# A planner's waiting times for non-urgent transfers, and new ordering weights for attention, in a hybrid DeltaNet and attention layer

## The chip, the cores and the metric

The kernel runs on one core of one Trainium2 chip, in one launch. The metric is the device time of one execution in microseconds. A core has five engines that matter here: PE (TensorE, matrix products and transposes), DVE (VectorE), ACT (ScalarE), POOL (GpSimd) and SP (SyncE, which here only issues the transfers). Each takes its instructions strictly in the order of its own program; an instruction that waits for something holds up all that stand behind it on that engine.

## The reference

One layer over 1024 latent tokens and 256 context tokens with 1024 channels, all in fp32:

```
h  = rms_norm(x) * (1 + scale) + shift            # scale, shift, gate from c
cols = h @ w_in                                   # q,k,v,z of branch A; q,k,v,z of branch B; gates
A: q,k,v = silu(centred_conv(.)); l2 norm of q, k; chunked gated delta rule, both directions, 8 heads
B: q,k = axial_rope(rms_norm(.)); attn = softmax(q0 k0) - lam * softmax(q1 k1); o = attn @ v, 8 heads
y  = rms_norm(o) * gain * silu(z)                 # for each branch
out = x + gate * ((g_a * (y_a @ w_oa) + g_b * (y_b @ w_ob)) @ w_out)
```

## The kernel before

**The planner.** The program is written by a planner in Python. Each piece of work is a generator (a "stream") that yields one operation at a time: the engine, an assumed duration, the tokens it depends on, and a function that emits the instruction. A token is a pair of engine and assumed end. `step` (line 127) keeps an assumed clock for each engine, for DMA the sum of the assumed transfer times with 2.5 us for the landing on top (`LAND`), and `turn_flow` and `flow` choose which stream goes next: the one that can start first by these clocks, with a bias for each stream. The order of choice is the order of the instructions on each engine. `later(t, us)` (line 229) returns a token whose assumed end is `us` later. It changes nothing that the chip waits for: the dependency itself stays as it was, only the place that the planner gives to the instruction in its engine's program moves.

**The stages**, with their times in the trace. Modulation, norm and the first products (0 to 60 us). The projections that feed the convolution, with convolution, norms and tables on the other engines (60 to 410): `gate_row` sums a gate row out of 16 transfers `graw`. The q, k, v projections of branch B, with the preparation of the first DeltaNet heads (410 to 745): `gdn_prep` loads `X` and `kq`, forms decays on ACT and Gram products on PE, solves 32x32 triangles on DVE from `ab`, merges them from `R`. The DeltaNet scan of both directions, with 32 output-gate projections as filler for PE (745 to 1310): `loads` fetches blocks `x` and masks them on POOL, `tails` norms a head's output with the gate `sz`. Attention (1350 to 1823), with the products `ma` of branch A (`merge_`) between. Then the products `mb` of branch B and the output projection (to 1993).

**Attention** works through 64 tiles of 128 queries (8 heads of 8). A tile: 12 score products `s` on PE, six pieces taken off by DVE (`score_out`, line 1560, tile `S`), exponentials on ACT (`soft`, 1573), scaling of the second map on ACT or POOL (`scale`, 1590 and 1592), the sum of both maps on POOL (`add`, 1597), ten transposes `t` on PE (`turns`), copies of high parts on ACT (`high`, 1629) and low parts on DVE (`low`, 1634), products `v` for pairs of tiles (`att_out`). After a pair, `gate_` (1671) multiplies by the gate `sz`. After the last pair of a head, `norm_` runs a chain: POOL takes a power into `bry` (179), PE transposes it into `m`, DVE copies it to `rt`, SP writes it to memory (`rbd<-rt`, 1715), SP reads it back to all partitions (`rr<-rbd`, 1717) once that has landed, POOL multiplies the head's output by it in four pieces (`oT`, 1720), SP stores it (`yb<-oT`). `merge_` takes one of 16 groups of 24 products `ma` at a time, loads its gate `g<-gt` (1791) as the group begins, and `merge_out` multiplies by it on DVE (1806). `att_load_ops` and `att_low_ops` load a later head by six transfers (`qh`, `kk`, `qh`, `kk`, `ql`, `ql`), called the head load below.

In attention every queue above is a stream with its own weight in `ABIAS`, and a due time that grows by one for each tile; a lower weight means that the stream is taken earlier. `flow`, which plans the DeltaNet stages, adds `FB0` or `FB1` to the filler's start, `FB0` while fewer than `FT` = 38 gate projections are done; there are 32 of them.

Of the kernel before, what the change touches and what calls it, by code (L numbers as in the profile page):

```python
# [17 lines left out]
P = 128  # L18
# [25 lines left out]
class Block:  # L44
# [427 lines left out]
    def first(self, done, right, late):  # L472

        self.head = self.late = None
        yield done
        for st in right:
            st.close()
        self.late = self.tk = late()
        self.gdn_first()
        g = self.preps(0)  # L480
        x = next(g)
        while x() if callable(x) else x[0] == DMA:
            x = next(g) if callable(x) else g.send((yield x))
# [175 lines left out]
    def gate_row(self):  # L659
# [24 lines left out]

# [398 lines left out]
    def gdn_prep(self, h):  # L1083
# [18 lines left out]
        for d in range(2):  # L1102
            for c in range(NT):
                t = yield ACT, 0.293, [ld], lambda: nc.scalar.activation(
                    X[:, d, c], X[:, d, c], AF.Abs, bias=self.gcc[:, c, d * H + h:d * H + h + 1], scale=-1.0)
            te[d] = yield ACT, 1.18, [t], lambda: nc.scalar.activation(X[:, d], X[:, d], AF.Exp, scale=-1.0), AF.Exp
# [45 lines left out]
        for j in range(31):  # L1152
            n, w = 31 - j, j + 1
            tv = tmp[:, :n * w].rearrange("p (a b) -> p a b", b=w)
            t = yield DV2, n * w / 960.0 + 0.08, [t, t1], lambda: V.tensor_tensor(  # L1155
# [9 lines left out]
        tt = yield DVE, 0.735, [tR], lambda: V.transpose(Rt, R)  # L1165
# [104 lines left out]
    def loads(self, d):  # L1270
# [3 lines left out]
        for h in range(H):  # L1274
            for c in order:
# [5 lines left out]
                if c < NL:  # L1281
                    u["tqk"] = yield POOL, 0.72, [u["tx"]], lambda: nc.gpsimd.tensor_tensor(  # L1282
# [77 lines left out]
    def tails(self):  # L1360
# [3 lines left out]
        for h in range(H):  # L1364
# [23 lines left out]
            for b0 in range(0, NL, 4):  # L1388
# [10 lines left out]
                sq = yield DVE, 0.663, [t1, ts], lambda: V.scalar_tensor_tensor(  # L1399
# [82 lines left out]
    FB1 = 0.71  # L1482
# [217 lines left out]
    def norm_(self, h, w, t, to):  # L1700
# [17 lines left out]
        for k in range(4):  # L1718
            s = slice(k * W, (k + 1) * W)
            t = yield POOL, 0.69, [e, to], lambda: nc.gpsimd.tensor_tensor(w["oT"][:, s], w["oT"][:, s], rr[:, s], ALU.mult)  # L1720
# [9 lines left out]
    def side_start(self):  # L1730
# [74 lines left out]
    def merge_out(self, o, m, g, tg, pt, t):  # L1805
        t = yield DVE, 0.605, [t, tg], lambda: self.nc.vector.tensor_tensor(g, pt, g, ALU.mult)
# [396 lines left out]
```

## Time and profile before

| what | before |
|---|---|
| median of 3 runs | 1991.84 us (1985.76 to 1995.66) |
| the profiled execution, its own time | 1994.94 us |
| its span, first to last instruction | 1993.2 us |
| busy in the span: PE, DVE, ACT, POOL | 1920.1, 1462.8, 1062.0, 680.2 us |
| mean granted clock of TensorE | 0.989 |
| DMA, mean over the span | 169 GB/s |

The own time of the profiled execution is 1.74 us above its span and 3.10 us above the median. In the views below, a row of the timeline gives start, length, engine, line, operation, out<-in and, in brackets, the idle time before it with what ended that; a row of the waits gives who waited for whom, the sum, how often and the longest; a row of the windows gives the busy time of each engine in a stretch, then the granted clock (PEclk), the busy share of the DMA engines and GB/s.

### The profile page before, as it was taken

The numbers are of one execution on the slowest core, as the hardware profiler recorded it, in microseconds if no ns is written. First come the engines' busy times: TensorE is split into PE (matmuls) and PEld (weight loads), VectorE is DVE, ScalarE is ACT, GpSimd is POOL, SyncE is SP. The second block draws the span as 40 slices with busy tenths as digits, with TensorE's granted clock in tenths as the row PEclk, the third lists the DMA queues.
The fourth block names the chain that finished last, engine by engine and source line by source line (L and its number), as shares of the span: only waits on it lengthen the run. The fifth ranks groups of instructions, "written<-read, shape, count | busy, mean of one in ns | idle before, by whom it ended". The sixth has DMA issues, their size and how long they took to land.

```text
span 1993.2 us, 37530 instructions
## 1 busy us (share of the span) xinstructions
PE 1920.1 (96%) x13807; PEld 1689.6 (85%) x13807; DVE 1462.8 (73%) x3613; ACT 1062.0 (53%) x2186; POOL 680.2 (34%) x610
## 2 busy tenths in 40 slices
PE   6999999999999999999999999999899999999999
PEld 4988888899999997888888888888879879898887
DVE  4787899847976986768866873346669788895677
ACT  4443335344325443677555655456658678684222
POOL 3200000014531332343433233334657476663203
PEclk9999999999999999999999999999999999999999
DMA  9145444576455456667587576575474665426542
GB/s 325 59 131 122 133 97 121 128 220 184 125 158 186 140 195 188 222 189 245 165 281 243 157 219 194 156 203 175 128 196 113 183 181 139 142 69 209 188 159 85
DMA packets 383038, 336.39 MB, mean 169 GB/s; under 512 B 142609, under 2 KB 323443, under 8 KB 381831
## 3 DMA queue, kind: packets, MB, share of 16 engines
q1 hardware_dynamic: 382855, 333.99, 56.4%
q8 instruction: 109, 1.79, 0.4%
q14 instruction: 74, 0.61, 0.1%
HBM read 222.14 MB, written 111.79 MB: 168 GB/s over the span
## 4 chain that ended last, share of the span: by engine, by line
PE 51%; DMA 6%; DVE 2%; POOL 1%; ACT 1%; issue 1%; SPq 1%; DVEq 0%; ACTq 0%; POOLq 0%
PE mm L56 15%; PE s L56 6%; PE chain L56 5%; PE v L56 5%; PE mb L56 4%; PE ma L56 3%; PE x L56 3%; PE t L63 3%; PE out L56 3%; DMA rbd<-rt 1%; DMA x<-xq 1%; DMA g<-gt 1%; PE gram L56 1%; PE pz L56 1%; PE z L56 1%
## 5 line engine op out<-in xcount | busy, mean ns | idle before, releaser
L56 PE MATMUL mm<-hs,wh 128*128 128x512 f32 (+1 forms) x2048 | 650.3, 391 | 1.5 <-DVE hs L408 1.4
L56 PEld LDWEIGHTS mm<-hs,wh 128*128 128x128 f32 x2048 | 372.2, 190 | 59.7 <-issue 2.3
L56 PE MATMUL mm<-hs,wl 128*128 128x512 f32 (+1 forms) x1024 | 397.6, 388 | 0.0
L56 PE MATMUL mm<-wh,hs 128*128 128x256 f32 (+1 forms) x1792 | 335.9, 287 | 1.0 <-issue 0.5
L56 PEld LDWEIGHTS mm<-wh,hs 128*128 128x128 f32 x1792 | 283.2, 193 | 1.7 <-ACT sq L978 0.7
L1560 DVE TENSOR_SCALAR_CACHE_REDUCE S<-s,rsq 128x512 f32<-128x512 f32 (+1 forms) x384 | 241.5, 655 | 29.0 <-PE s L56 24.5
L56 PE MATMUL mm<-wl,hs 128*128 128x256 f32 (+1 forms) x896 | 256.7, 286 | 0.0
L56 PEld LDWEIGHTS mm<-hs,wl 128*128 128x128 f32 x1024 | 194.3, 190 | 27.9 <-DVE wl L886 0.2
L1597 POOL TENSOR_TENSOR S<-S 128x1280 f32<-128x1280 f32 x64 | 189.3, 2962 | 75.3 <-ACT S L1590 72.1
L1573 ACT ACTIVATE S<-S,mn 128x1280 f32<-128x1280 f32 x128 | 175.3, 1370 | 44.7 <-DVE mn L1572 43.7
L56 PEld LDWEIGHTS mm<-wl,hs 128*128 128x128 f32 x896 | 172.6, 193 | 0.0
L56 PE MATMUL s<-kk,qh 128*128 128x512 f32 (+1 forms) x384 | 145.5, 379 | 5.9 <-DVE S L1560 5.8
L595 DVE SCALAR_TENSOR_TENSOR ac<-xc,convT,ac 128x1284 f32<-128x1284 f32 (+1 forms) x96 | 138.4, 1446 | 12.4 <-ACT ac L593 11.9
L56 PE MATMUL s<-kk,ql 128*128 128x512 f32 (+1 forms) x384 | 135.4, 362 | 0.0
L1634 DVE TENSOR_TENSOR al<-t,ah 128x512 fp32r<-128x512 f32 (+1 forms) x192 | 108.1, 595 | 36.3 <-ACT ah L1629 36.1
L1155 DVE TENSOR_TENSOR tmp<-ab,ts 80x31 f32<-80x31 f32 (+15 forms) x248 | 98.0, 395 | 12.4 <-DMA ab<-da 6.7
L580 POOL MEMSET xc<- 128x2 f32 (+1 forms) x64 | 3.6, 101 | 299.5 <-DMA gkk<-xc 128.2
L1629 ACT CAST ah<-t 128x512 fp32r<-128x512 f32 (+1 forms) x192 | 91.7, 518 | 26.5 <-PE v L56 12.6
L63 PE MATMUL t<-ct,S 128*128 128x128 f32 x640 | 97.0, 277 | 4.4 <-POOL S L1597 2.0
L1157 DVE TENSOR_TENSOR ts<-ts,tmp 80x31 f32<-80x31 f32 (+15 forms) x248 | 93.4, 376 | 5.6
L1318 ACT ACTIVATE vd<-chain,edk 128x128 f32<-128x128 f32 x144 | 52.4, 369 | 81.6 <-PE chain L56 80.5
L1282 POOL TENSOR_TENSOR x<-x,ct 128x256 f32<-128x256 f32 x64 | 49.0, 770 | 131.1 <-DMA x<-xq 95.8
(296 smaller groups left out, 4401.4 us busy)
## 6 DMA issues: line engine op xcount, KB each, us to landing
wr<-in_w_in_dram SPq DMA_DIRECT2D x48, 512.0 KB
hx<-in_w_in_dram SPq DMA_DIRECT2D x64, 256.0 KB
x<-xq SPq DMA_DIRECT2D x64, 256.0 KB
X<-gcd SPq DMA_DIRECT2D x8, 1280.0 KB
kd<-col SPq DMA_DIRECT2D x40, 256.0 KB
xq<-X SPq DMA_DIRECT2D x16, 640.0 KB
kk<-kd SPq DMA_DIRECT2D x16, 640.0 KB
kq<-gkq SPq DMA_DIRECT2D x8, 1152.0 KB
```

Of the source, the lines that this page charges most:

```text
L56: self.nc.tensor.matmul(out, lhsT, rhs, start=start, stop=stop)
L63: self.nc.tensor.transpose(out, src, self.ident[:src.shape[0], :src.shape[0]])
L595: t = yield DV2, 1.21e-3 * wd, [t], lambda: nc.vector.scalar_tensor_tensor(ac[:, :wd], xc[:, j:j + wd], self.convw(j, x["ct"]), ac[:, :wd] ...
L1155: t = yield DV2, n * w / 960.0 + 0.08, [t, t1], lambda: V.tensor_tensor(tv, ab[:, j + 1:, j:j + 1].to_broadcast([80, n, w]), ts[:, j, :w]. ...
L1157: t = yield DV2, n * w / 960.0 + 0.08, [t, t1], lambda: V.tensor_tensor(ts[:, j + 1:, :w], ts[:, j + 1:, :w], tv, ALU.subtract)
L1282: u["tqk"] = yield POOL, 0.72, [u["tx"]], lambda: nc.gpsimd.tensor_tensor(x[:, 1], x[:, 1], (self.up, self.lo)[d].unsqueeze(1).to_broadcas ...
L1318: td = yield ACT, 0.251, [t], lambda: nc.scalar.activation(vd, pc[:, 1], AF.Copy, scale=self.edk[:, c, g:g + 1])
L1560: e = yield DVE, 0.675 if m == 512 else 0.408, [e, self.sfree[c].get(n - 4 + c)], lambda: self.nc.vector.tensor_scalar(x["S"][c][:, o:o + ...
L1573: x["x"].append((yield ACT, 1.36, [e], lambda: nc.scalar.activation(S, S, AF.Exp, bias=x["mn"][:, c:c + 1], scale=-1.0, accum_out=w["l0"][ ...
L1597: e = yield POOL, 2.9, [e], lambda: self.nc.gpsimd.tensor_tensor(S0, S0, S1, ALU.add)
L1629: e = yield ACT, 0.48 if nb == 4 else 0.27, [t, y["old", k]], lambda: self.nc.scalar.copy(y["ah", k][:, :, q], pv)
L1634: t = yield DVE, 0.603 if k < 2 else 0.322, [e, y["old", k]], lambda: self.nc.vector.tensor_tensor(y["al", k][:, :, q], pv, y["ah", k][:, ...
```

## The change

Nine kinds of operation that consume a transfer get a later place by `later`: the Gram products and their partners behind `kq` (1.5 us), the decays on ACT behind `X` (2.0), the first step of the triangles behind `ab` (2.5), the transpose behind `R` (2.5), the masks on POOL behind `x` (1.0), the gated norm of branch A behind `sz` (1.5), the gate of attention behind its `sz` (2.0), the multiplications `oT` on POOL behind `rr` (4.0), and the multiplication on DVE behind `g` (3.0). The allowance for `graw` goes from 6.0 to 4.0. The rope table `tb` is fetched before the first preparation, not after it. Five of the weights in `ABIAS` are new, and `FB1` goes from 0.71 to 0.36.

```diff
@@ first
         self.late = self.tk = late()
+        tb = self.tk.tile([P, 2, 2, NL, 32], F32, tag="tb", name="tb")
+        self.rope["k"] = tb, (yield DMA, 1.5, [], lambda: self.nc.sync.dma_start(..., self.tbd[1]))
         self.gdn_first()
...
-        tb = self.tk.tile([P, 2, 2, NL, 32], F32, tag="tb", name="tb")
-        self.rope["k"] = tb, (yield DMA, 1.5, [], lambda: self.nc.sync.dma_start(..., self.tbd[1]))
@@ gate_row
-                e = self.later(e, 6.0)
+                e = self.later(e, 4.0)
@@ gdn_prep
-            tk = tq = yield DMA, 3.3, self.kT_t, lambda: nc.sync.dma_start(kq, self.gkq[h])
+            tk = yield DMA, 3.3, self.kT_t, lambda: nc.sync.dma_start(kq, self.gkq[h])
+            tk = tq = self.later(tk, 1.5)
...
-                t = yield ACT, 0.293, [ld], lambda: nc.scalar.activation(
+                t = yield ACT, 0.293, [self.later(ld, 2.0)], lambda: nc.scalar.activation(
...
-            t = yield DV2, n * w / 960.0 + 0.08, [t, t1], lambda: V.tensor_tensor(
+            t = yield DV2, n * w / 960.0 + 0.08, [t if j else self.later(t, 2.5), t1], lambda: V.tensor_tensor(
...
-        tt = yield DVE, 0.735, [tR], lambda: V.transpose(Rt, R)
+        tt = yield DVE, 0.735, [self.later(tR, 2.5)], lambda: V.transpose(Rt, R)
@@ loads
-                    u["tqk"] = yield POOL, 0.72, [u["tx"]], ...
+                    u["tqk"] = yield POOL, 0.72, [self.later(u["tx"], 1.0)], ...
@@ tails
-                sq = yield DVE, 0.663, [t1, ts], ...
+                sq = yield DVE, 0.663, [t1, self.later(ts, 1.5)], ...
@@
-    FB1 = 0.71
+    FB1 = 0.36
@@ gate_
-        y["o"] = yield DVE, 0.345, [t, self.kept.get(h - 2), w["tsz"]], ...
+        y["o"] = yield DVE, 0.345, [t, self.kept.get(h - 2), self.later(w["tsz"], 2.0)], ...
@@ norm_
-            t = yield POOL, 0.69, [e, to], lambda: nc.gpsimd.tensor_tensor(w["oT"][:, s], w["oT"][:, s], rr[:, s], ALU.mult)
+            t = yield POOL, 0.69, [self.later(e, 4.0), to], lambda: nc.gpsimd.tensor_tensor(w["oT"][:, s], w["oT"][:, s], rr[:, s], ALU.mult)
@@
-    ABIAS = dict(rels=-0.59, softs=10.8, norms=5.82, gateq=-13.3, sums=-14.54,
+    ABIAS = dict(rels=-0.59, softs=8.84, norms=5.82, gateq=-27.29, sums=-14.54,
...
@@ merge_out
-        t = yield DVE, 0.605, [t, tg], lambda: self.nc.vector.tensor_tensor(g, pt, g, ALU.mult)
+        t = yield DVE, 0.605, [t, self.later(tg, 3.0)], lambda: self.nc.vector.tensor_tensor(g, pt, g, ALU.mult)
```

In the rest of the table `outs` goes from -50.16 to -42.85, `highs` from -18.9 to -9.33 and `att_out` from 4.51 to 8.18.

**Where instructions stand now.** The first place is SP's program around the norm chain of the first head (`rbd<-rt`, `rr<-rbd`); `qh`, `kk` and `ql` are a head load, `wq` weights, `ma` and `g` belong to the groups of `merge_`. Before:

```order
L1498 DMA kk<-kd 64x2x1280
L1506 DMA ql<-qd 64x2x1024 x2
L1808 DMA ma<-g 128x512
L1791 DMA g<-gt 128x512
L1715 DMA rbd<-rt 8x128
L1767 DMA wq<-in_w_oa_dram 128x4x128 x2
L1717 DMA rr<-rbd 128x1024
L1525 DMA vh<-vd 128x4x128
```

In the changed kernel the same place reads:

```order
L1698 DMA sz<-szb 128x1024
L1808 DMA ma<-g 128x512
L1791 DMA g<-gt 128x512
L1715 DMA rbd<-rt 8x128
L1717 DMA rr<-rbd 128x1024
L1767 DMA wq<-in_w_oa_dram 128x4x128 x2
L1726 DMA yb<-oT 128x1024
L1497 DMA qh<-qd 64x2x1024
```

The write and the read of the norm chain stood behind a head load, and stand ahead of it now. Over all eight heads, `rbd` stands right behind a head load (with only `ma` and `g` between) for heads 0 and 2 before and for none now, and a head load stands between `rbd` and `rr` for head 4 before and for head 3 now.

The second place is POOL's program from the first head's `bry` to the second head's; `S<-S` is the sum of a tile's two maps, `wl` the low part of a weight of branch A. Before:

```order
L179 TENSOR_TENSOR bry<-ms,mhalf 128x8
L1592 TENSOR_TENSOR S<-S,rl 128x1280
L1597 TENSOR_TENSOR S<-S 128x1280 x3
L1777 TENSOR_TENSOR wl<-wq,wh 128x512
L1597 TENSOR_TENSOR S<-S 128x1280
L1777 TENSOR_TENSOR wl<-wq,wh 128x512
L1720 TENSOR_TENSOR oT<-oT,rr 128x256 x4
L179 TENSOR_TENSOR bry<-ms,mhalf 128x8
```

In the changed kernel:

```order
L179 TENSOR_TENSOR bry<-ms,mhalf 128x8
L1597 TENSOR_TENSOR S<-S 128x1280
L1777 TENSOR_TENSOR wl<-wq,wh 128x512 x2
L1597 TENSOR_TENSOR S<-S 128x1280
L1720 TENSOR_TENSOR oT<-oT,rr 128x256 x4
L1597 TENSOR_TENSOR S<-S 128x1280
L1592 TENSOR_TENSOR S<-S,rl 128x1280
L1597 TENSOR_TENSOR S<-S 128x1280 x2
L1777 TENSOR_TENSOR wl<-wq,wh 128x512 x2
L1597 TENSOR_TENSOR S<-S 128x1280 x3
L179 TENSOR_TENSOR bry<-ms,mhalf 128x8
```

Before, the second head's `bry` stood right behind the first head's `oT`, and now six sums stand between. Before, `bry` of heads 1, 3 and 5 stood at most two instructions behind an `oT`; now that of head 4 does, with two `wl` between.

The third place is DVE's program around the first multiplication by `g`; the rows of line 1560 take score pieces off, 60 of them ahead of `g` before and 59 now. Before:

```order
L1560 TENSOR_SCALAR S,m_15776<-s,rsq 128x512
L1560 TENSOR_SCALAR S,m_15776<-s,rsq 128x256
L1572 TENSOR_REDUCE mn<-m_15776 128x1
L1581 RECIPROCAL rl<-l_15666 128x1
L1806 TENSOR_TENSOR g<-ma,g 128x512
L1583 TENSOR_SCALAR rl<-rl,l_15666,neglam 128x1
L1560 TENSOR_SCALAR S,m_15864<-s,rsq 128x512 x2
```

In the changed kernel:

```order
L1572 TENSOR_REDUCE mn<-m_15813 128x1
L1560 TENSOR_SCALAR S,m_15813<-s,rsq 128x512
L1806 TENSOR_TENSOR g<-ma,g 128x512
L1560 TENSOR_SCALAR S,m_15813<-s,rsq 128x256
L1560 TENSOR_SCALAR S,m_15859<-s,rsq 128x512
L1581 RECIPROCAL rl<-l_15663 128x1
```

Counted in score pieces the multiplication has hardly moved; on PE, though, a whole group of 24 products `ma` and 70 transposes now stand ahead of the 60th score piece, where 12 and 60 stood before.

More of the change, by code (lines that the diff above doesn't have):

```diff
@@ L478, in first @@
         self.late = self.tk = late()
+        tb = self.tk.tile([P, 2, 2, NL, 32], F32, tag="tb", name="tb")
+        self.rope["k"] = tb, (yield DMA, 1.5, [], lambda: self.nc.sync.dma_start(tb.rearrange("p a b t f -> p (a b t f)"), self.tbd[1]))
         self.gdn_first()
@@ L483, in first @@
             x = next(g) if callable(x) else g.send((yield x))
-        tb = self.tk.tile([P, 2, 2, NL, 32], F32, tag="tb", name="tb")
-        self.rope["k"] = tb, (yield DMA, 1.5, [], lambda: self.nc.sync.dma_start(tb.rearrange("p a b t f -> p (a b t f)"), self.tbd[1]))
         self.head = g, x
@@ L1281, in loads @@
                 if c < NL:
-                    u["tqk"] = yield POOL, 0.72, [u["tx"]], lambda: nc.gpsimd.tensor_tensor(
+                    u["tqk"] = yield POOL, 0.72, [self.later(u["tx"], 1.0)], lambda: nc.gpsimd.tensor_tensor(
                         x[:, 1], x[:, 1], (self.up, self.lo)[d].unsqueeze(1).to_broadcast([P, 2, P]), ALU.mult)
@@ L1398, in tails @@
                     t1 = yield PE, 0.109, [t, b], lambda: self.tr(pt[:, j * P:(j + 1) * P], oa[:, b0 + j])
-                sq = yield DVE, 0.663, [t1, ts], lambda: V.scalar_tensor_tensor(
+                sq = yield DVE, 0.663, [t1, self.later(ts, 1.5)], lambda: V.scalar_tensor_tensor(
                     ov, pt, self.gdn_g, sz, ALU.mult, ALU.mult)
@@ L1670, in gate_ @@
         yield lambda: "tsz" in w
-        y["o"] = yield DVE, 0.345, [t, self.kept.get(h - 2), w["tsz"]], lambda: self.nc.vector.scalar_tensor_tensor(
+        y["o"] = yield DVE, 0.345, [t, self.kept.get(h - 2), self.later(w["tsz"], 2.0)], lambda: self.nc.vector.scalar_tensor_tensor(
             w["oT"][:, s], po[:, :W], self.dg, w["sz"][:, s], ALU.mult, ALU.mult)
@@ L1743 @@
     PACE = 4.48
-    ABIAS = dict(rels=-0.59, softs=10.8, norms=5.82, gateq=-13.3, sums=-14.54,
-                 outs=-50.16, lows=-2.4, highs=-18.9, adds=26.02, scales=31.0, evs=22.29, mouts=-3.31,
-                 att_out=4.51, turns=3.19, scores=-12.11, merge=1.0)
+    ABIAS = dict(rels=-0.59, softs=8.84, norms=5.82, gateq=-27.29, sums=-14.54,
+                 outs=-42.85, lows=-2.4, highs=-9.33, adds=26.02, scales=31.0, evs=22.29, mouts=-3.31,
+                 att_out=8.18, turns=3.19, scores=-12.11, merge=1.0)
     KEEP = 3
```

## The prediction

> **What bounds the kernel now.** I read the page first, then the windows by stage, then the waits of PE, and last the timelines around the longest of them. The page and the windows say that PE sets the time almost everywhere (the columns are the stretch, then the busy time of PE, its weight loads, DVE, ACT and POOL, the clock, DMA).
>
> ```profile
> PE 1920.1 (96%) x13807; PEld 1689.6 (85%) x13807; DVE 1462.8 (73%) x3613; ACT 1062.0 (53%) x2186; POOL 680.2 (34%) x610
> ```
>
> ```profile
> 60.00:410.00 350.00, 347.85 (x1868) 299.68 (x1867) 295.80 (x444) 147.67 (x186) 7.92 (x69) 1.00 0.47 119
> ...
> 745.00:1310.00 565.00, 547.40 (x4736) 474.71 (x4735) 368.52 (x1054) 326.19 (x958) 192.45 (x248) 0.99 0.66 206
> ...
> 1350.00:1823.00 473.00, 450.91 (x2874) 398.27 (x2873) 376.11 (x1247) 347.26 (x584) 284.16 (x143) 0.97 0.55 151
> 1823.00:1993.00 170.00, 166.25 (x722) 134.91 (x720) 114.02 (x131) 41.05 (x51) 36.94 (x22) 1.00 0.46 154
> ```
>
> So only PE's idle time can be won: 17.6 us in the scan (565 - 547.40) and 22.1 in attention (473 - 450.91), which also has the lowest clock, 0.97. The waits of PE say for whom (sum, times, longest):
>
> ```profile
> PE m L63 <- POOL bry L179: 10.6, 3, 6.4
> ...
> PE s L56 <- DVE S L1560: 5.8, 4, 5.0
> ...
> PE t L63 <- POOL S L1597: 2.0, 1, 2.0
> ...
> PE t L63 <- DVE al L1634: 1.8, 3, 1.4
> PE gram L56 <- DVE X L1127: 1.8, 1, 1.8
> ...
> PE gram L56 <- DMA kq<-gkq: 1.3, 1, 1.3
> ```
>
> The first and the third come through POOL. Its timeline shows that it stood still itself, each time ahead of `oT`, for the transfer `rr`, with `bry` of the next head right behind:
>
> ```profile
> 1473.96 2.79 POOL L1720 TENSOR_TENSOR oT<-oT,rr 128x256 f32<-128x256 f32 x4 [13.78 <-DMA rr<-rbd]
> 1476.71 1.64 POOL L179 TENSOR_TENSOR bry<-ms,mhalf 128x8 f32<-128x8 f32 x1
> ...
> 1592.61 2.79 POOL L1720 TENSOR_TENSOR oT<-oT,rr 128x256 f32<-128x256 f32 x4 [15.05 <-DMA rr<-rbd]
> ...
> 1702.02 2.84 POOL L1720 TENSOR_TENSOR oT<-oT,rr 128x256 f32<-128x256 f32 x4 [10.35 <-DMA rr<-rbd]
> ```
>
> SP shows why `rr` was late. The small write `rbd` stood behind a head load: issued at 1455.94, it let `rr` go at 1469.29, 13.35 us later; with nothing large ahead it took at most 3.8 us (1480.11 to 1483.88). The third time `rr` itself stood behind a head load, issued at 1685.07 and used at 1702.02.
>
> ```profile
> 1451.81 1.25 SPq L1506 DMA_DIRECT2D ql<-qd  x2
> ...
> 1455.94 0.29 SPq L1715 DMA_DIRECT2D rbd<-rt  x1
> ...
> 1469.29 0.34 SPq L1717 DMA_DIRECT2D rr<-rbd  x1
> ...
> 1480.11 0.45 SPq L1715 DMA_DIRECT2D rbd<-rt  x1
> ...
> 1483.88 0.33 SPq L1717 DMA_DIRECT2D rr<-rbd  x1
> ...
> 1683.75 1.28 SPq L1506 DMA_DIRECT2D ql<-qd  x2
> 1685.07 0.59 SPq L1717 DMA_DIRECT2D rr<-rbd  x1
> ```
>
> The second wait in the list is DVE's: it stood 7.64 us for `g`, which landed 16.50 us after its issue, also behind a head load, and PE lost 5.02 us. These are PE's rows at the four stalls, then DVE's at its wait and the chain's row of that transfer:
>
> ```profile
> 1405.44 0.80 PE L56 MATMUL s<-kk,qh 128*128 128x512 f32 x1 [5.02 <-DVE S L1560]
> ...
> 1478.40 0.27 PE L63 MATMUL m<-ct,bry 128*8 128x128 f32 x1 [3.58 <-POOL bry L179]
> ...
> 1599.48 0.38 PE L63 MATMUL m<-ct,bry 128*8 128x128 f32 x1 [6.40 <-POOL bry L179]
> ...
> 1724.78 2.09 PE L63 MATMUL t<-ct,S 128*128 128x128 f32 x10 [1.98 <-POOL S L1597]
> ```
>
> ```profile
> 1403.85 0.69 DVE L1806 TENSOR_TENSOR g<-ma,g 128x512 f32<-128x512 f32 x1 [7.64 <-DMA g<-gt]
> ```
>
> ```profile
> 1387.25 16.50 DMA g<-gt
> ```
>
> Each stall costs more than its gap, since the clock drops for some microseconds after it (second last but one column, 1.00 is full speed):
>
> ```profile
> 1405.00:1410.00 5.00, 4.56 (x17) 4.17 (x18) 4.02 (x16) 4.52 (x7) 3.30 (x3) 0.50 0.51 154
> 1410.00:1415.00 5.00, 5.00 (x30) 4.51 (x29) 2.12 (x6) 3.82 (x8) 2.33 (x2) 0.89 0.21 59
> ...
> 1480.00:1485.00 5.00, 5.00 (x19) 4.00 (x18) 3.73 (x15) 2.00 (x4) 4.65 (x3) 0.72 0.88 289
> ...
> 1600.00:1605.00 5.00, 5.00 (x20) 3.82 (x19) 4.83 (x20) 2.76 (x4) 3.15 (x2) 0.77 0.98 359
> ...
> 1725.00:1730.00 5.00, 5.00 (x28) 4.78 (x27) 1.61 (x8) 1.54 (x2) 5.00 (x3) 0.66 0.56 177
> ```
>
> Five microseconds times the missing share: 2.5 + 0.55 = 3.1 us after the stall at 1405, 1.4 at 1480, 1.2 at 1600, 1.7 at 1725.
>
> **The change part by part.** No instruction is added or removed that computes anything, and no dependency changes; every term is a matter of place.
>
> *The norm chain (`oT` 4.0 us later, the new weights).* It costs PE now 10.6 (`m`) + 2.0 (`t`) in gaps and 1.4 + 1.2 + 1.7 in clock: 16.9 us. In the changed program `rbd` of heads 0 and 2 stands ahead of the head load, so both stalls of over 13 us on POOL lose their cause, and the next `bry` stands six sums further on. What stays is one head, now head 3, whose `rr` stands behind a head load, with `bry` of head 4 soon behind its `oT`. That is head 4's case of today, worth the 0.6 us that the list leaves for the third `m` (10.6 - 3.58 - 6.40), 1.98 and 1.7: 4.3 us. Gain 16.9 - 4.3 = 12.6. The ends are 0, if POOL waits just as long elsewhere, and 16.9. I take 12.6, as its row is the same arrangement. Queued behind the moved `oT` on POOL are sums for PE's transposes, on SP the store `yb` and behind it a head load or the next `v` loads; those must not run late, and a head load has the rest of its head for that.
>
> *`g` on DVE (3.0 us later).* It costs 5.02 + 3.1 = 8.1 us now. The head load and `g` keep their place on SP, so the landing stays; the planner allows the multiplication 3.0 us more, and PE has 12 more products and 10 more transposes ahead of it, so DVE comes to it some 3 us later. DVE then waits 7.64 - 3.0 = 4.6 us, PE 5.02 - 3.0 = 2.0, and the clock drops as after the 1.98 us gap, 1.7. Gain 8.1 - 3.7 = 4.4; ends 0 and 8.1.
>
> On the clock there is a rule to weigh. By the Trainium skill ("TensorE: Matmul & The Clock Gate", Part 1: The HAM clock gate) the clock halves after an idle window of about 3.4 us. By it, gaps of 2 us would cost no clock, and the two remainders of 1.7 us would go too, 3.4 us more gain. The row at 1725 stands against it: the clock was 0.66 after a gap of 1.98, so I keep both remainders.
>
> *`kq`, `X`, `tb`, `ab`, `R`, `x`, both `sz`.* The waits on these transfers are here (POOL, DVE and ACT for whom, sum, times, longest):
>
> ```profile
> POOL x L1282 <- DMA x<-xq: 95.8, 29, 12.8
> ```
>
> ```profile
> DVE tmp L1155 <- DMA ab<-da: 6.7, 4, 2.5
> ```
>
> ```profile
> ACT X L1104 <- DMA X<-gcd: 6.2, 3, 3.5
> ```
>
> Of what PE waits for, only the two `gram` rows, 1.8 + 1.3 = 3.1 us, hang on them; I count half, 1.5 (ends 0 and 3.1). The 95.8 us of POOL are long but idle: POOL is busy for 192 of the 565 us there, and no wait of PE names `x`'s mask. So the scan counts 0. Its order is made anew throughout, and PE's 17.6 us of idle there bound the gain; I let it go from a gain of 5 to a loss of 6.
>
> *`graw`, `FB1`.* Between 60 and 410 us PE stops for 2.15 us in all (350 - 347.85), so an earlier place for `graw` is worth 0; if it is too early, DVE waits for the landing under PE's work, with 54 us of its own to spare there (350 - 295.80). `FB1` is never read, as at most 32 projections are done and `FT` is 38: 0.
>
> *The new weights.* Where no transfer interferes, PE has nothing to win from another order, so here I look for cost. The nearest row is a transpose that waited for DVE's low parts, with the clock behind it:
>
> ```profile
> 1362.19 0.44 PE L63 MATMUL t<-ct,S 128*128 128x128 f32 x2 [1.38 <-DVE al L1634]
> ```
>
> ```profile
> 1360.00:1365.00 5.00, 3.40 (x17) 2.21 (x16) 3.37 (x10) 1.72 (x4) 0.00 (x0) 0.83 0.97 263
> 1365.00:1370.00 5.00, 5.00 (x32) 4.79 (x31) 4.07 (x16) 2.98 (x4) 0.00 (x0) 0.83 1.03 379
> ```
>
> That is 1.4 + 0.85 + 0.6 = 2.8 us for one. I charge one; the ends are none and five, 0 and 14.
>
> *The sum:* -12.6 - 4.4 - 1.5 + 0 + 2.8 = -15.7 us. The profiled execution's 1994.94 becomes 1979.2; it lies 3.1 above the median, so the forecast for the median is 1991.84 - 15.7 = 1976 us.
>
> **The rivals.** *R1, the wait stays with the transfer.* The bytes and their order on the queue are what makes `g` and `rr` late; an instruction that asks later finds the same landing, and POOL's and DVE's waits come back at other heads, as they did at head 4 with another arrangement. For it: the head load is still ahead of `g` at 1387 and of `rr` at one head. Against it: `rbd` has moved ahead of the head load at two. It leaves a quarter of the gain, 4 us: 1988. The Trainium skill ("DMA: Bandwidth & Descriptors", Queues, rings and completion order) says that each DMA engine works through its descriptors in order and that a completion lands only after all earlier writes of that engine; the 13.35 us of a write that else took 3.8 agree.
>
> *R2, no room between `bry` and `m`.* In the new program PE's transpose `m` of heads 1, 3 and 5 stands inside the ten transposes of the very tile whose sum POOL makes just before `bry`. Any lateness of POOL then stops PE directly, as at 1478 and 1599. For it: POOL is 60% busy in attention (284 of 473), with bursts. Against it: the three stalls came from POOL's waits, not from its work. Three waits of 2 us with 1.7 us of clock are 11 us: 1987.
>
> *R3, slower.* `highs` is less urgent by 9.6, so ACT puts exponentials ahead of the copies that free the transposes' banks, and PE stops for `al`, 2.8 us each time. It decides from the sixth time on (15.7 / 2.8 = 5.6, beside the one charged). For it: the row at 1362 exists. Against it: with the present weights such waits come to 1.8 us in three. At twelve of 64 tiles more it costs 34 us, and the time is 1976 + 34 = 2010.
>
> **How the numbers follow.** The forecast has 0.55 with a range of its own from 1962 to 1985, R1 0.17, R2 0.17, R3 0.09; that the order change does nothing at all, 0.02. A measurement of this kernel can tell about 0.5%, 10 us, from no change: faster means below 1982, slower above 2002. Of the forecast's 0.55 about 0.05 lies above 1982; R1 and R2 add 0.05 to faster, the rest of them to same. That makes faster 0.55, same 0.36, slower 0.09. The range reaches from all gains at their upper ends less a little (16.9 + 8.1 + 3.1 = 28, that is 1964, and 2 for the scan) to R1 and R2 with a few microseconds on top: 1962 to 1994, leaving out R3 and some 0.1 at the ends.
>
> **What would show it.** Right: no wait of POOL over 5 us for `rr` but one, near `bry` of head 4; PE's waits for `bry` down from 10.6 to about 1; DVE's wait for `g` at about 4.6 us and PE's gap there near 2; a clock of 0.98 or more in attention, and a stage that is 15 us shorter from its first score to the first `mb`; the other stages within 6 us. Wrong: POOL's waits for `rr` still at some 40 us in long pieces (R1); new gaps ahead of `m` with POOL busy (R2); `t` waiting for `al` or ACT for tens of microseconds (R3); a scan that is longer by over 6 us.

## The result, and the profile after

The changed kernel takes 1965.41 us (median; 1962.13 to 1966.65), beside 1990.80 us (1985.76 to 1995.66) for the kernel before in all its runs: a ratio of 0.987, 95% interval 0.984 to 0.990, about 25 us less. The forecast was 1976 with a range from 1962 to 1994. So the sign and the range held, the latter with 3 us to spare at its lower end, and the gain was 10 us larger than the sum. The profiled execution has an own time of 1966.57 us, a span of 1964.8 and a mean clock of 0.996.

Two stages became fuller. These are windows of the changed kernel by stage (busy time of PE, its weight loads, DVE, ACT and POOL, then clock, DMA share and GB/s):

```profile
410.00:745.00 335.00, 332.51 (x3219) 327.69 (x3218) 264.17 (x646) 146.90 (x335) 119.18 (x90) 1.00 0.55 175
745.00:1310.00 565.00, 547.77 (x4720) 473.91 (x4719) 367.57 (x1054) 333.04 (x962) 189.94 (x247) 0.99 0.69 210
1350.00:1823.00 473.00, 462.93 (x2930) 406.04 (x2929) 388.12 (x1258) 349.12 (x586) 286.76 (x147) 0.99 0.58 161
```

The last row's stretch starts 8 us behind the changed kernel's attention and takes in 28 us of the next stage, so attention is better measured between two marks: PE's first transpose `t` and the first product `mb`. The kernel before has this row for the first stage, and these two for the marks (behind the durations, the first and the last start):

```profile
410.00:745.00 335.00, 324.54 (x3141) 319.39 (x3140) 255.25 (x622) 143.81 (x329) 117.14 (x88) 0.99 0.54 171
```

```profile
L63 PE MATMUL t<-ct,S x640: 270/272/421, 1357.4 to 1805.9; 128*128 128x128 f32 x160
```

```profile
L56 PE MATMUL mb<-yh,wh x128: 393/396/399, 1823.1 to 1912.0; 128*128 128x512 f32 x128
```

And this is how the two marks stand after:

```profile
L63 PE MATMUL t<-ct,S x640: 270/272/446, 1342.0 to 1778.7; 128*128 128x128 f32 x160
```

```profile
L56 PE MATMUL mb<-yh,wh x128: 393/396/399, 1794.7 to 1883.6; 128*128 128x512 f32 x128
```

Attention starts 15.4 us earlier (1357.4 - 1342.0). From its first `t` to the first `mb` it takes 452.7 us instead of 465.7, 13.0 less. About half of the gain is thus where the prediction saw it, and the other half ahead of attention, where it had counted 1.5 us.

Between the two marks PE runs the same 2840 instructions in both kernels, so the 13.0 us can be split. PE's idle time fell from 22.1 to 12.1 us. What the lower clock cost (half of PE's busy time in the stretches that the trace has at half clock) fell from 9.3 to 3.4. The rest, the net time that PE takes for these instructions, rose from 434.2 to 437.3. Below, "net time" means this rest.

In attention the waits of PE read so (sum, times, longest); its wait for `bry`, first in the list before, has no row left:

```profile
PE s L56 <- DVE S L1560: 2.9, 6, 1.9
...
PE v L56 <- DVE oT L1671: 2.6, 4, 1.0
PE t L63 <- DVE al L1634: 2.6, 3, 1.8
...
PE t L63 <- POOL S L1597: 1.4, 1, 1.4
```

POOL still waits for `rr`, at heads 1, 3 and 7, but only at head 3 with a `bry` soon behind, as foreseen (the first row is head 1, whose next `bry` comes 22 us later):

```profile
1496.35 2.83 POOL L1720 TENSOR_TENSOR oT<-oT,rr 128x256 f32<-128x256 f32 x4 [3.46 <-DMA rr<-rbd]
...
1618.78 2.83 POOL L1720 TENSOR_TENSOR oT<-oT,rr 128x256 f32<-128x256 f32 x4 [12.21 <-DMA rr<-rbd]
...
1624.07 1.65 POOL L179 TENSOR_TENSOR bry<-ms,mhalf 128x8 f32<-128x8 f32 x1
```

SP shows that this `rr` stands behind a head load, issued at 1600.13 and used at 1618.78:

```profile
1598.64 1.45 SPq L1506 DMA_DIRECT2D ql<-qd  x2
1600.13 0.60 SPq L1717 DMA_DIRECT2D rr<-rbd  x1
```

DVE's wait for `g` is 2.53 us and PE's gap behind it 1.89, then the one gap that POOL's late sum leaves (DVE's row, then PE's two):

```profile
1387.32 0.69 DVE L1806 TENSOR_TENSOR g<-ma,g 128x512 f32<-128x512 f32 x1 [2.53 <-DMA g<-gt]
```

```profile
1388.47 0.39 PE L56 MATMUL s<-kk,qh 128*128 128x256 f32 x1 [1.89 <-DVE S L1560]
...
1631.08 0.44 PE L63 MATMUL t<-ct,S 128*128 128x128 f32 x2 [1.35 <-POOL S L1597]
```

### The profile page after: what moved, and what is told of

It is laid out like the page before. It is cut to its first block, busy times and chain, and to the rows that moved or that the text cites. A ratio compares the mean times of both kernels' runs of the same rounds, so it can differ in the third digit from the quotient of the medians.

```text
span 1964.8 us, 37491 instructions
## 1 busy us (share of the span) xinstructions
PE 1909.4 (97%) x13807; PEld 1679.4 (85%) x13807; DVE 1465.1 (75%) x3613; ACT 1069.4 (54%) x2191; POOL 677.4 (34%) x610
## 3 DMA queue, kind: packets, MB, share of 16 engines
q8 instruction: 109, 1.79, 0.4%
## 4 chain that ended last, share of the span: by engine, by line
PE 77%; DVE 8%; DMA 7%; ACT 3%; issue 2%; SPq 1%; POOL 1%; DVEq 0%; ACTq 0%; POOLq 0%
PE mm L56 38%; PE s L56 6%; PE v L56 6%; PE chain L56 5%; PE mb L56 5%; PE ma L56 4%; PE x L56 3%; PE t L63 3%; PE out L56 2%; DVE S L1560 1%; PE gram L56 1%; DMA vv<-gv 1%; DVE ac L595 1%; PE pz L56 1%; DMA g<-gt 1%
## 5 line engine op out<-in xcount | busy, mean ns | idle before, releaser
L1629 ACT CAST ah<-t 128x512 fp32r<-128x512 f32 (+1 forms) x192 | 91.9, 518 | 32.6 <-PE t L63 15.3
L1157 DVE TENSOR_TENSOR ts<-ts,tmp 80x31 f32<-80x31 f32 (+15 forms) x248 | 97.5, 393 | 6.1
L56 PE MATMUL v<-ah,vh 128*128 128x256 f32 x320 | 93.0, 291 | 0.0
```

Of the source, the lines that this page charges most:

```text
L56: self.nc.tensor.matmul(out, lhsT, rhs, start=start, stop=stop)
L1629: e = yield ACT, 0.48 if nb == 4 else 0.27, [t, y["old", k]], lambda: self.nc.scalar.copy(y["ah", k][:, :, q], pv)
```

## The experiments

All were timed in rounds beside the kernel before, whose medians in the three groups were 1992.66 (first four runs), 1989.56 (next four) and 1991.94 us (last four). The last columns are from each run's profile.

| run | what is changed | median us | ratio to before, 95% | PE busy 410 to 745 | first `t` | first `t` to first `mb` |
|---|---|---|---|---|---|---|
| before | | 1990.80 | | 324.54 | 1357.4 | 465.7 |
| after | all | 1965.41 | 0.987 (0.984 to 0.990) | 332.51 | 1342.0 | 452.7 |
| e1_flow | all ahead of attention | 1976.52 | 0.993 (0.990 to 0.995) | 332.84 | 1339.7 | 466.3 |
| e2_attention | all of attention | 1980.19 | 0.994 (0.992 to 0.996) | 325.31 | 1351.8 | 451.3 |
| e3_weights | the weights alone | 2006.51 | 1.008 (1.006 to 1.010) | 325.71 | 1352.9 | 480.4 |
| e4_allowances | attention's allowances alone | 2003.85 | 1.007 (1.005 to 1.010) | 325.47 | 1351.5 | 476.6 |
| e5_table | `tb` alone | 1989.64 | 0.9995 (0.998 to 1.001) | 325.67 | 1356.8 | 462.1 |
| e6_grams | `kq` and `X` | 1974.38 | 0.992 (0.990 to 0.994) | 330.74 | 1335.4 | 467.8 |
| e7_inverse | `ab` and `R` | 1986.56 | 0.998 (0.997 to 1.000) | 327.76 | 1353.7 | 464.4 |
| e8_no_g | after, `g` without allowance | 1967.37 | 0.989 (0.986 to 0.991) | 332.82 | 1339.5 | 455.6 |
| e9_kq | `kq` alone | 1990.98 | 1.000 (0.998 to 1.001) | 325.62 | 1360.5 | 465.2 |
| e10_X | `X` alone | 1980.74 | 0.994 (0.992 to 0.997) | 329.10 | 1341.2 | 465.8 |
| e11_no_rr | after, `rr` without allowance | 1989.99 | 0.999 (0.998 to 1.000) | 332.92 | 1336.7 | 477.8 |
| e12_fewer | `kq`, `X` and all of attention | 1979.69 | 0.994 (0.992 to 0.996) | 328.46 | 1342.1 | 465.7 |

The runs e2 to e4 have the program of before up to attention, and e1, e8 and e11 that of the changed kernel: in their traces DVE, ACT and POOL have the same order up to there. So there are four profiles of each. The first `t` comes at 1351.5 to 1357.4 us with the early program of before (mean 1353.4) and at 1336.7 to 1342.0 with that of the changed kernel (mean 1339.5). One profile alone is uncertain by some 5 us, and the early stages are about 14 us shorter. Ahead of that mark PE is idle for 45.3 to 47.3 us in the first four and for 37.8 to 39.5 in the others, and the clock costs 4.6 to 8.5 and 1.7 to 3.4 us.

### The early half: e1_flow

The edits are the place of `tb` and the allowances of `graw`, `kq`, `X`, `ab`, `R`, `x` and of branch A's `sz`; attention's three allowances and the weights stay as before.

```diff
-                e = self.later(e, 6.0)
+                e = self.later(e, 4.0)
...
+            tk = tq = self.later(tk, 1.5)
...
-                t = yield ACT, 0.293, [ld], lambda: nc.scalar.activation(
+                t = yield ACT, 0.293, [self.later(ld, 2.0)], lambda: nc.scalar.activation(
```

> Only the edits of the stages up to the scan (rope table, graw, kq, X, ab, R, x, sz of branch A); attention's weights and allowances as before. The two traces put 15.4 us of the gain ahead of the first transpose t of attention (1357.4 us before, 1342.0 after) and 13.0 us between it and the first product mb (465.7 before, 452.7 after). Theory (each stage keeps its own gain): first t at 1342 us, attention 465 us, time about 1975 us. Rival (the gain ahead of attention is only work that attention hands over or takes on): attention longer by as much as the first part is shorter, time about 1988 us.

Measured: 1976.52 us, 14.5 less than before by its ratio (interval 9.8 to 19.3). Attention stays as it was (466.3 us), and the waits that hurt there stay as well (POOL's, PE's, DVE's of this run):

```profile
POOL oT L1721 <- DMA rr<-rbd: 61.0, 7, 17.0
...
PE m L63 <- POOL bry L179: 12.6, 3, 6.4
...
DVE g L1807 <- DMA g<-gt: 7.8, 1, 7.8
```

So the half that the prediction had put at 1.5 us is worth more than 9.

### The attention half: e2_attention

The three allowances of attention, the five weights and `FB1`; everything ahead of attention as before.

```diff
-            t = yield POOL, 0.69, [e, to], lambda: ...
+            t = yield POOL, 0.69, [self.later(e, 4.0), to], lambda: ...
...
-        t = yield DVE, 0.605, [t, tg], lambda: ...
+        t = yield DVE, 0.605, [t, self.later(tg, 3.0)], lambda: ...
```

> Only attention's edits (allowances for oT behind rr, for g and for sz, the new weights, FB1); everything ahead of attention word for word as before. Theory (each stage keeps its own gain): first t at 1357 us, attention 453 us, time about 1978 us; POOL waits for rr once for over 10 us, at head 3. Rival (attention's gain hangs on the earlier stages' new order): attention 460 us or more, time 1985 us or more.

Measured: 1980.19 us, 11.5 less by its ratio (interval 8.0 to 15.3), with attention at 451.3 us. The waits are those of the changed kernel: no row of PE for `bry`, `v` behind the gate 2.6 us in four, `g` 3.0 in two. The two halves add up to 26.0, and together they gave 25; with another early part they don't add up (e12 below).

### The weights alone and the allowances alone: e3_weights and e4_allowances

```diff
-    ABIAS = dict(rels=-0.59, softs=10.8, norms=5.82, gateq=-13.3, sums=-14.54,
+    ABIAS = dict(rels=-0.59, softs=8.84, norms=5.82, gateq=-27.29, sums=-14.54,
```

is e3 (with the rest of the table); e4 has the three allowances of attention with the old table.

> Only the five new weights; no allowance. In this program rbd of head 0 already stands ahead of the head load, that of head 2 behind one, and rr of head 4 behind one. Theory W (what counts is where the write stands on SP, which the weights set): the wait for rr of head 0 goes, those of heads 2 and 4 stay, attention 460 us, time about 1985 us. Theory A (what counts is the allowance of 4 us for oT): attention as before, 466 us or more, time about 1991 us.

> Only attention's three allowances (oT behind rr 4.0 us, g 3.0, sz 2.0), with the old weights. In this program rbd of head 0 still stands behind a head load. Theory W: POOL still waits about 10 us for rr of head 0, attention 460 to 466 us, time about 1988 us. Theory A: oT stands so far back that the waits cost nothing, attention 455 us, time about 1980 us. In both, DVE's wait for g falls from 7.6 us to about 4.6.

Both are slower than before, by 16 us (11 to 21) and 15 us (10 to 20), and neither expectation had that. Each takes away part of the old stalls: PE waits for `bry` 3.8 us in the first and has no such row in the second. In e3 POOL stands where its theory W had it, not at head 0, but for 11 us ahead of `oT` at heads 2 and 4 (at head 2 the trace names the transfer `vl`); the time is not that theory's. Each run gets new gaps. In e3 (waits of PE, DVE and ACT):

```profile
PE v L56 <- DVE oT L1671: 10.6, 8, 4.8
...
PE t L63 <- DVE al L1634: 7.3, 4, 5.0
...
DVE g L1806 <- DMA g<-gt: 5.5, 1, 5.5
ACT yh L1872 <- DMA yl<-yb: 5.5, 3, 4.9
```

PE's 5.0 us for `al` are the old stall for the first `g`: DVE waits 5.5 us for the transfer, and that `al` stands right behind. The longest new gap in both, 4.78 and 5.01 us, lies close to attention's end. ACT stands still for the load `yl` of the next stage, ahead of the square `osq` on which attention's last `v` hangs (ACT of e3):

```profile
1812.09 1.04 ACT L1872 CAST yh<-yl 128x1024 fp32r<-128x1024 f32 x1 [4.94 <-DMA yl<-yb]
...
1815.66 0.38 ACT L1664 ACTIVATE osq<-v 128x256 f32<-128x256 f32 x1
```

That is once more an operation with a non-urgent transfer in front of an urgent one on an in-order engine, in a place where the change has put no allowance. In the changed kernel ACT waits for `yl` too (6.7 us in seven pieces), but PE's gap there is 0.93.

The new gaps are not the whole loss. Attention is 14.7 us longer than before in e3: 7.7 more of idle time, 2.7 of clock and 4.3 of PE's net time. In e4 it is 10.9: 3.8, 0.9 and 6.2. In seven profiles with the old attention (before, e1, e5, e6, e7, e9, e10) the net time is 433.7 to 434.7 us, in the seven with any edit to it 436.8 to 440.4. Why the same instructions take PE longer in another order was not tried.

### What rr's allowance is worth beside the new weights: e11_no_rr

```diff
-            t = yield POOL, 0.69, [self.later(e, 4.0), to], lambda: ...
+            t = yield POOL, 0.69, [e, to], lambda: ...
```

> The changed kernel with the 4.0 us allowance of rr taken away; the weights and g's allowance stay. The prediction's price of this term, 12.6 us: POOL waits over 10 us for rr at two or three heads with bry behind, PE stops for bry some 10 us, 1977. Rival, from the run with the weights alone, in which head 0's wait was gone without the allowance: the weights have moved the write rbd ahead of the head load already, POOL waits once, 3 to 5 us slower than the changed kernel, 1969.

Measured: 1989.99 us. Against the ratio of the changed kernel (0.999 and 0.987) that is 24 us, twice the price of the prediction. These are five windows of attention's second half in the changed kernel, and then the same in e11 (the last one reaches 20 us into the changed kernel's next stage):

```profile
1540.00:1600.00 60.00, 59.60 (x400) 53.27 (x398) 53.67 (x183) 50.50 (x87) 40.73 (x18) 1.00 0.78 209
1600.00:1660.00 60.00, 58.30 (x373) 51.47 (x373) 47.44 (x159) 43.32 (x70) 39.28 (x23) 1.00 0.58 152
1660.00:1720.00 60.00, 59.19 (x401) 52.67 (x401) 52.45 (x176) 49.41 (x86) 40.52 (x21) 1.00 0.54 141
1720.00:1780.00 60.00, 58.81 (x381) 50.64 (x381) 51.73 (x171) 46.90 (x81) 38.51 (x20) 1.00 0.25 77
1780.00:1815.00 35.00, 34.07 (x164) 27.96 (x163) 19.38 (x27) 13.04 (x18) 4.49 (x6) 1.00 0.77 263
```

```profile
1540.00:1600.00 60.00, 56.35 (x336) 47.83 (x334) 43.31 (x143) 38.48 (x63) 36.02 (x22) 0.94 0.72 219
1600.00:1660.00 60.00, 59.42 (x398) 52.14 (x397) 54.89 (x190) 52.00 (x90) 39.28 (x17) 1.00 0.58 141
1660.00:1720.00 60.00, 55.17 (x335) 47.52 (x335) 45.69 (x154) 39.34 (x65) 37.31 (x23) 0.97 0.52 141
1720.00:1780.00 60.00, 55.57 (x375) 49.91 (x374) 52.32 (x175) 49.00 (x85) 37.96 (x18) 0.97 0.24 76
1780.00:1815.00 35.00, 28.01 (x150) 23.63 (x149) 17.48 (x24) 14.53 (x24) 11.56 (x8) 0.90 0.60 196
```

PE is idle for 20.5 us in e11 and for 5.0 us after, 15.5 more. The clock's missing shares are 3.6 + 1.8 + 1.8 + 3.5 = 10.7 us against none. Together that is 26, and attention is 25.1 us longer by its marks (477.8 - 452.7). Of e11's 20.5, the norm chain has 2.52 and 1.23 (`m` behind `bry`) and 3.17 (`t` behind POOL's sum), 6.9 in all; `v` behind the gate has 8.8 in five gaps, among it 5.05 us in the same place as in e3:

```profile
1797.82 1.01 PE L56 MATMUL v<-ct,osq 128*128 128x1 f32 x4 [5.05 <-DVE oT L1671]
```

The rival (POOL waits once, 4 us) is wrong, and the price of 12.6 is wrong too, though the part of it in the norm chain is of the expected kind: POOL stands for 11.1 us ahead of `oT` at heads 2 and 4 (at head 2 the trace names the transfer `vl`), with `bry` right behind. The allowance decides which arrangement of the whole second half the planner finds, and that is worth more than the wait.

### What g's allowance is worth: e8_no_g

```diff
-        t = yield DVE, 0.605, [t, self.later(tg, 3.0)], lambda: ...
+        t = yield DVE, 0.605, [t, tg], lambda: ...
```

> The changed kernel with the 3.0 us allowance of g taken away; only g moves, one place ahead on DVE, and six products of v move behind it on PE. The prediction's price: DVE waits for g some 3 us longer (2.5 -> 5), PE's gap 1.9 -> about 4.6 and the clock 1.4 us worse: 4.4 us slower than the changed kernel, 1970. Rival: with the new weights PE has other work at hand there, or the wait moves whole: within 1.5 us of 1965.4.

Measured: 1967.37 us, 2 us above the changed kernel by the medians and 3.6 by the ratios, whose intervals overlap. The wait is there in the expected size and a little more (DVE's row, then PE's, of e8):

```profile
1385.35 0.69 DVE L1806 TENSOR_TENSOR g<-ma,g 128x512 f32<-128x512 f32 x1 [6.18 <-DMA g<-gt]
```

```profile
1386.51 0.66 PE L63 MATMUL t<-ct,S 128*128 128x128 f32 x2 [5.73 <-DVE al L1634]
```

PE's gap is 3.8 us longer, and attention 2.9. That agrees with the prediction's 4.4 as far as it can be told.

### Which early edit it is: e5_table, e6_grams, e7_inverse, e9_kq, e10_X

e5 has only the two moved lines of `tb`; e6 the allowances of `kq` and `X`, e9 and e10 one of them each; e7 has

```diff
-            t = yield DV2, n * w / 960.0 + 0.08, [t, t1], lambda: V.tensor_tensor(
+            t = yield DV2, n * w / 960.0 + 0.08, [t if j else self.later(t, 2.5), t1], lambda: V.tensor_tensor(
...
-        tt = yield DVE, 0.735, [tR], lambda: V.transpose(Rt, R)
+        tt = yield DVE, 0.735, [self.later(tR, 2.5)], lambda: V.transpose(Rt, R)
```

> Only the load of the table tb is issued first of its stage; attention and the scan keep their order. Theory S (every stall of PE between 410 and 745 us has one load behind it): the waits of PE's tr for DVE's fin, which is made from tb, go (1.39 + 1.90 + 0.44 us, and some 2.5 us of clock), and the two waits of gram stay; PE busy in the stage 324.5 -> about 330 of 335, the time 6 us shorter, 1987. Theory P (the stalls come from where DVE and ACT stand in the plan of the whole stage, and only all allowances together move them): fin's waits stay or move, PE busy within 2 us of 324.5, the time within 2 us of the kernel before.

> Only the allowances of kq (1.5 us) and X (2.0 us). Theory S: the two gram waits go (1.79 + 1.27 us and 1.7 us of clock behind the first), fin's waits stay, PE busy in the stage about 329, and the time is 5 us shorter, 1988; the scan's order is made anew and stays within 3 us. Theory P: the gram waits are replaced by others, PE busy 323 to 327, time within 3 us of before.

> Only the allowances of ab and R (2.5 us each), which feed the inverses of the scan. Theory S: PE's two stops ahead of the products of RR and Z (1.70 us at 595 and 3.31 us at 788, with some 3.4 us of clock) shrink to about 0.6 each, 5 to 7 us shorter, 1986; gram's and fin's waits stay. Theory P: other gaps of the same size take their place, within 3 us of before.

> Only the allowance of kq (1.5 us), the load that the products gram and the bodies of the scan read. Theory K (the gain of the two allowances together, 15 us, is kq's: it shifts the whole scan in the plan, and the products that fill in come elsewhere): 10 to 13 us shorter, 1978, with PE busy in the scan up by 5 us. Theory G (each allowance takes away its own gap of gram and no more): PE's gap of 1.27 us for kq goes, the other stays, 1 to 3 us shorter, 1987.

> Only the allowance of X (2.0 us); the scan and attention keep their order. Theory K: the first gram gap of 1.79 us goes, 2 to 3 us shorter with its clock, 1987. Theory G, with the stalls of fin hanging on X too, since ACT and DVE stop for X ahead of them: 5 to 8 us shorter, 1983.

`tb` gives nothing, with the waits for `fin` all in place. `kq` alone gives nothing. `ab` and `R` give 3 us (0.6 to 6): the two stops of PE that the expectation names are gone, but the scan as a whole is idle for 19.7 us, more than before (565 - 545.29). `X` alone gives 11 us (7 to 15), and with `kq` it is 16 (11 to 21). That is the size of the whole early half, 14.5 in e1, so what the other early edits add can't be told from nothing.

The difference between 11 and 16 can't be put down to `kq` either. In the traces of e10 and e6 DVE, ACT, POOL and SP have one and the same order, and PE's differs in one place only, a group of `gram` at 487 us, where e10 waits 0.85 us for `kq`. The expectations of e9 and e10 had the roles the wrong way round. With `kq` alone the scan keeps the order of before on DVE, ACT, POOL and SP; it is `X` that makes it anew, though its expectation says that the scan keeps its order. The windows rows of e10 for the stage and the scan, beside 324.54 and 547.40 before, and then those of e6:

```profile
410.00:745.00 335.00, 329.10 (x3194) 324.56 (x3193) 257.32 (x635) 144.76 (x332) 118.73 (x89) 0.99 0.55 175
745.00:1310.00 565.00, 551.13 (x4751) 476.60 (x4751) 356.23 (x1040) 330.41 (x961) 189.31 (x248) 1.00 0.66 204
```

```profile
410.00:745.00 335.00, 330.74 (x3210) 325.65 (x3209) 261.35 (x644) 144.73 (x332) 120.97 (x90) 1.00 0.55 175
745.00:1310.00 565.00, 553.01 (x4762) 479.04 (x4761) 354.38 (x1031) 332.70 (x965) 188.15 (x248) 1.00 0.66 207
```

In e10 PE is busy for 4.6 us more in the stage and 3.7 more in the scan, in e6 6.2 and 5.6. Between 60 and 1340 us the clock's missing shares come to 1.7 us, with 8.6 before and 5.1 in each of e2 to e4, which have the program of before. Behind the last transposes `oT` of the scan stand 107 products of the projections fewer than before, since they are now done inside it, and these 36.8 us instead of 59.3 look like a gain of 22. They are none by themselves: ahead of the first `t` PE runs 10247 instructions in both, and what the scan takes in makes it longer (its last `oT` start at 1304.4 us, and at 1298.1 before). Only the idle time that they fill counts, and the clock. In e1 and in the changed kernel the scan wins nothing (547.77, beside 547.40), and the stage from 410 to 745 is 8 us fuller.

Theory S of e5 to e7 (each gap has its load) fails in its plainest case, `tb`, and theory P fails in e6. What those gaps have behind them is in the trace of before. DVE around the first of them:

```profile
444.68 0.42 DVE L1000 TENSOR_TENSOR fin<-fin,sq 128x256 f32<-128x256 f32 x1
...
446.81 2.50 DVE L1000 TENSOR_TENSOR fin<-fin,sq 128x256 f32<-128x256 f32 x1
449.23 0.41 DVE L1124 TENSOR_TENSOR qk<-gram,X 128x256 f32<-128x256 f32 x1
449.67 0.61 DVE L1127 SCALAR_TENSOR_TENSOR X<-gram,beta,X 128x128 f32<-128x128 f32 x2
```

The same `fin` takes 0.42 us, and here 2.50. The next rows wait for nothing but it, and PE's `gram` (1.79 us) waits for them. POOL ran this at that time:

```profile
446.45 2.56 POOL L886 TENSOR_TENSOR wl<-wr,wh 128x1024 fp32r<-128x1024 f32 x1
```

It is the same at the two longer waits of `tr` in that stage, 1.39 us at 645 (a `fin` of 2.62 us beside a `wl` of 2.38) and 1.90 at 708 (DVE, then POOL, then PE):

```profile
705.31 2.59 DVE L1000 TENSOR_TENSOR fin<-fin,sq 128x256 f32<-128x256 f32 x1
```

```profile
705.27 2.35 POOL L886 TENSOR_TENSOR wl<-wr,wh 128x1024 fp32r<-128x1024 f32 x1
```

```profile
707.96 1.11 PE L63 MATMUL tr<-ct,fin 128*128 128x128 f32 x4 [1.90 <-DVE fin L1000]
```

So 5.1 of that stage's 10.5 us of gaps were no late transfer at all, but two-input additions on DVE that ran beside a POOL instruction. Of the three gaps one is left in the changed kernel, of 1.10 us, behind a `fin` of 2.63:

```profile
637.14 2.63 DVE L998 TENSOR_TENSOR fin<-raw,hx 128x256 f32<-128x256 f32 x1
```

The slow `fin` have not gone: another takes 2.64 us at 540 beside a `wl` of 2.40, and PE has no gap behind it. So what changed is whether PE had other work at hand. No run takes POOL's instruction away, so this rests on the rows alone.

### A version with fewer edits: e12_fewer

`kq`, `X` and all of the attention half, without the other early edits.

> Of the early part only the allowances of kq and X, with all of the attention part; tb, graw, ab, R, x and the scan's sz as before. If the gains add up: 1974.4 of kq and X, less 12.5 of the attention part, 1962, or 3 us faster than the changed kernel. Rival: the weights fit the start of attention that the changed kernel has; with another start one or two stalls come back, 1968 to 1974.

Measured: 1979.69 us, 14 more than the changed kernel. The rival is right and too mild: attention takes 465.7 us, no less than before. Part of the stalls is gone, with PE idle for 17.8 us (22.1 before) and 7.7 lost to the clock (9.3), but PE's net time is 440.2 us, 6.0 longer. POOL waits for `rr` 44.4 us in four, with heads 0 and 4 ahead of a `bry` again, and PE for `m` 2.3 and for DVE's `S` 5.2 us. Its start of attention is the changed kernel's (1342.1 and 1342.0), so the time of that start alone doesn't decide it; what else of the early order does was not tried. No version tried beats the changed kernel.

## Why the prediction was right, and where it was not

**The norm chain, gain 12.6.** Right in its mechanism: `rbd` moved ahead of the head loads, the long waits at heads 0 and 2 went, head 3 kept one. The remainder was 1.35 us of `t` and no `m` behind `bry`, not 4.3. One reading was too narrow: "at most 3.8 us" from the issue of `rbd` to that of `rr`, with no head load ahead, holds for the pair that is shown, but other heads of the same trace have 2.0 to 6.7 (6.71 at head 3, 1603.03 to 1609.74). As a price of the allowance 12.6 was too small: without it the changed kernel loses 24 us (e11).

**g on DVE, gain 4.4.** Right: DVE's wait is 2.5 us (4.6 forecast), PE's gap 1.89 (2.0), and e8 gives 2 to 4 us.

**The new weights, a charge of 2.8.** Wrong as a term of its own. By themselves they cost 16 us (e3), the allowances by themselves 15 (e4), and together they gain 11.5 (e2). The step that failed is the one that gave each its price in the trace of before and added the prices. The sum of both terms and the charge, 14.2, came close to the 11.5 of e2 and the 13.0 of attention's marks. The charge is of the right size by luck: `t` behind `al`, from which it was worked out, rose by 0.8 us only (1.8 to 2.6), while PE's net time, which has no term in the prediction, rose by 3.1. R3 shows in no run: of the 7.3 us of `t` behind `al` in e3 5.0 are the stall for `g`, and the 2.3 left are near the 1.8 of before.

**kq, X, tb, ab, R, x, sz: 1.5 us, the scan 0.** This is where the missing 10 us are: 14.5 measured (e1), and `X` alone has most of it. The step that failed is "of what PE waits for, only the two `gram` rows hang on them". It named the loads from the releaser's name. The first `gram` row named `X`, but the rows of DVE show that `X` was late through a slow `fin`, not through its load. The rows of `tr` behind `fin`, 3.7 us, were not counted. And a later place for `X` on ACT makes the order anew behind it, which no price of a single gap can hold. The scan, put at 0 with 5 as the best end, won 3.7 us of idle time in e10 and none in the changed kernel, within these ends. In the changed kernel PE's idle time from 410 to 745 us is 8 us less; over all that stands ahead of attention, by the four profiles of each program, idle time is some 8 us less and the clock some 3. The remaining 3 of the 14 are PE's net time.

That the time fell inside the range is in part luck: the range's lower end was worked out from attention's terms at their best, 3.1 for the early part and 2 for the scan, while attention gave less than its sum and the early part gave 14.

**graw and FB1: 0.** Nothing speaks against it; neither was tried alone, but e2 has the new `FB1` and keeps the order of before up to attention.

**The rivals.** R1 is wrong: POOL's waits for `rr` stay at half (29.9 us in three, 60.5 in seven before), but of PE's time they cost only the 1.35 us. R2 is wrong in the changed kernel: no `m` waits for `bry`. In e11 and e12 `m` waits for it again, 2.5 and 2.35 us, but there POOL had stood ahead of `oT` for 11 and 12 us just before, which is the old stall and not a POOL that is busy with its own work.

**What would show it.** POOL over 5 us once near a `bry`: yes, and once at the last head, where nobody waits. PE's wait for `bry` near 1: none. DVE for `g` 4.6: 2.5. Clock in attention 0.98: 0.99. Attention 15 us shorter from its first score: 13.0 from the first `t`. The other stages within 6 us: no, about 14.

## What to carry to other kernels

Where a planner sets the order, an allowance and the weights that were chosen with it are one edit: price them together, or not at all, since here two losses of 15 us made a gain of 11.5. Before a gap of PE is put down to a transfer, follow the releaser one row further on its own engine and compare that row's duration with others of its kind. Work that a stage takes in from the stage behind it wins only as much as it fills of that stage's gaps; so measure to a mark that has the same instructions ahead of it in both kernels, and split the time there into idle time, clock and the rest.

## What the runs showed of the hardware

Some of DVE's two-input instructions lengthen beside POOL's. In the trace of before, 51 DVE instructions took over 0.3 us longer than the median of their kind (line, operation and operand shapes), 45 of them with two inputs. Each of the 51 overlapped a POOL instruction, and the excess from 410 to 745 us is 15.7 us, in the scan 25.8. But 804 two-input instructions overlapped one, so most stay as they are: `fin` beside POOL's powers of 128x8, which last 1.7 us, takes 0.43 us. The Trainium skill ("SBUF — State Buffer", SBUF: two separate sides) says that DVE and GpSimd share a pair of ports, which one instruction holds to its end; the 2.50 to 2.62 us of `fin` beside 2.35 to 2.56 of `wl` agree, and the 0.43 beside a power doesn't. The excess is not what the change won: in the changed kernel it is 15.2 us in the stage and 25.3 in the scan, as before. In e10 the scan's is 19.0, with 11 us won, and in e7 16.1, with 3.

The clock doesn't drop behind every gap of about 2 us. In the trace of before, a gap of 1.90 us for `fin` was followed by 0.80 and 0.86, 1.7 us lost; in e2, with the same program up to there and a gap of 1.91, the clock stayed at 1.00 (windows of before, then of e2):

```profile
705.00:710.00 5.00, 3.10 (x19) 2.89 (x19) 3.14 (x3) 0.59 (x1) 2.62 (x2) 0.80 0.89 299
710.00:715.00 5.00, 5.00 (x38) 5.00 (x38) 4.62 (x11) 4.32 (x14) 1.74 (x1) 0.86 0.81 311
```

```profile
700.00:705.00 5.00, 3.09 (x27) 2.89 (x25) 4.02 (x5) 0.54 (x2) 3.81 (x2) 1.00 0.94 300
705.00:710.00 5.00, 5.00 (x44) 5.00 (x43) 4.44 (x10) 4.68 (x15) 1.74 (x1) 1.00 0.98 365
```

So part of what the prediction charged to gaps as clock, 1.7 us each, is chance in one profile. What decides it can be read from the traces. Their record of the granted clock has stretches of 3.41 us, or two of these in a row, at half clock, which is 1.7 us lost for each that is busy. In the trace of before there are ten between 60 us and the last product, and all begin on one grid of 3.41 us. In the piece of the grid ahead of each, PE was idle for 1.6 to 3.4 us; pieces with up to 1.8 us of idle time left the clock at 1.00. The gap of 1.90 us lay whole in one piece, and that of 1.91 in e2 was cut by the grid, with 1.46 us idle in the larger part. The Trainium skill ("TensorE: Matmul & The Clock Gate", Part 1: The HAM clock gate) says that the window is free-running, and the grid agrees; its condition of an idle window of about 3.4 us isn't met by a gap of 1.90, and here about half of that was enough.
